# RWKV-7 main loop: the small output products of a group of four chunks behind the products for N, instead of one pair in each state step

## The chip, the cores and the metric

The kernel runs on one core of one Trainium2 chip. The metric is the device time of one execution in microseconds (us), lower is better. Before the change three executions took 1460.63, 1456.24 and 1459.01 us, median 1459.01.

The engines are named as the profile names them: PE is TensorE (matrix products), PEld its weight loads, DVE is VectorE, ACT is ScalarE, POOL is GpSimd, SP issues most of the DMAs. PSUM is the memory into which TensorE writes; here it has eight banks, four of them for large projections (tiles `dp`) and four for everything else (pool `mx`).

## The reference

The program is one layer of a decoder: an input projection, three mixers side by side (HGRN2, a dilated-window attention, RWKV-7), an output projection, a gated MLP and a gated embedding. Only the RWKV-7 mixer matters here. Its recurrence, per head of width 64 over 1024 positions, is

```
def step(state, inp):
    r_t, w_t, k_t, v_t, kk_t, a_t = inp
    sa = jnp.einsum('bhvk,bhk->bhv', state, -kk_t)
    state = (state * w_t[:, :, None, :] + sa[..., None] * (kk_t * a_t)[:, :, None, :]
             + v_t[..., None] * k_t[:, :, None, :])
    return state, jnp.einsum('bhvk,bhk->bhv', state, r_t)
```

with four heads. `y`, the second result, is then normalised, gated and passed on to the output projection.

## The kernel before

The recurrence is computed in chunks of 64 positions, 16 chunks in a row. Two heads make a pair that fills the 128 partitions, so the loop runs twice (p = 0 and p = 1, the first and the second head pair). `rwkv_groups` handles four chunks at a time, groups g = 0 to 3. For a group it computes what does not need the state for all four chunks together, and then walks through four state steps u = 0 to 3, chunk c = 4g + u.

Around the steps these tiles matter:

- `W` holds, per chunk and head, two 128x64 blocks: slot 0 makes the part of the output that comes from inside the chunk, slot 1 the part of the next state that does. `XV` holds the corrected values. Both are complete before the products for N.
- `pn` (L958): eight products `W[.., 1, :]` by `XV`, 64x64 results, two heads by four chunks. VectorE scales them into `N` (L959).
- `GM`: per chunk a 128x256 matrix, of which columns 128 to 255 carry the state on and columns 0 to 127 turn the state into output. VectorE writes it in two halves of two chunks (L949).
- One state step: `pS = GM . S` (L975), then on VectorE `S' = pS * gC + N` (L976). For the output: a pair of products `W[.., 0, :]` by `XV`, one for each head, into `pyo` (L978), and `GM . S` added to it (L980).
- In group 0 step 0 has no state: `S` is a copy of `N` (L971), and there is only the pair. Chunk 15 has no pS.

Between the steps TensorE is given other work by hand: `fill(1)` takes the next three products (128x512) of a projection that belongs to a later stage (L130, L132, L134); `inverse_first` (L872) starts the inverse of the next group, `values_turn` transposes the next group's v (L844). After a group, `place` copies the transposed v into XV on ScalarE (L851), which must wait until all readers of the old XV are through, and `result` copies `pyo` out of its bank (L885). Then come the scores of the next group, `sc` (L903), and `pu` (L914).

The loop stands under `manual_schedule` for TensorE, VectorE, ScalarE and GpSimd, so the order there is the order of the code; pieces of a later projection are put between by a scheduler (the weight splits L106 and L108 and some L130 to L134). The four banks of pool `mx` are handed out as tiles are asked for: which bank a tile gets, and thus whom it waits for, follows from the tiles before it.

Of the kernel before, what the change touches and what calls it, by code (L numbers as in the profile page):

```python
# [10 lines left out]
F32 = mybir.dt.float32  # L11
# [7 lines left out]
P = 128  # L19
# [60 lines left out]
class Trunk:  # L80
# [708 lines left out]
    def rwkv_groups(self, p, rp, d, y3, steps):  # L789

        nc, mxp = self.nc, self.mxp
        ar, v, gC = d["ar"], d["v"], d["gC"]
        msk = self.msk.rearrange("p (m h i) -> p m h i", h=2, i=64)
        Q = slice(0, 64), slice(64, 128)

        def rt(name, shape, bufs=1):
            return rp.tile(shape, F32, tag=name, name=self.nm(name), bufs=bufs)

        def fill(k):
            for _ in range(k):  # L800
                next(steps)
# [13 lines left out]
        def quad(name, g):  # L815
            t[name, g] = w = rt(name, [P, 4, P])
            nc.vector.tensor_tensor(w.rearrange("p u (o i) -> p u o i", i=32),
                                    d[name][:, group(g), :].unsqueeze(2).broadcast_to([P, 4, 4, 32]),
                                    self.qmask.rearrange("p (o i) -> p o i", i=32).unsqueeze(1).broadcast_to([P, 4, 4, 32]),
                                    ALU.mult)  # L820
# [12 lines left out]
        def add_ar(g):  # L833
            nc.gpsimd.tensor_copy(add[:, :, 0, :], ar[:, group(g), 1, :])
# [18 lines left out]
        X, GM = rt("X", [P, 4, P]), rt("GM", [P, 4, 256])  # L853
        GM5 = GM.rearrange("p u (a h i) -> p u a h i", a=2, h=2)
        W, XV = rt("W", [P, 4, 2, 2, 64]), rt("XV", [P, 4, 2, 64])
# [12 lines left out]
        def inverse_first(g):  # L868
            t["Y"] = rt("Y", [P, 4, P])
            py = mxp.tile([P, 4, P], F32, tag="mx", name=self.nm("py"))  # L870
            for u in range(4):
                nc.tensor.matmul(py[:, u, :], t["AB", g][:, u, :], t["T", g][:, u, :], start=True, stop=True)  # L872
            nc.scalar.copy(t["Y"], py)
            if g < 3:
                scores_bd(g + 1)

        def values_turn(g):
            t["pv"] = turn(lambda b: v[:, 256 * g + P * b:256 * g + P * b + P])
# [8 lines left out]
        S, before = None, None  # L887
# [3 lines left out]
        for g in range(4):  # L891
# [55 lines left out]
            def gm(us):  # L947
                for h, q in enumerate(Q):
                    nc.vector.tensor_tensor(GM5[q, us, :, h, :], pg[q, us], add[q, us], ALU.add)  # L949
# [8 lines left out]
                    nc.tensor.matmul(pn[q, u, :], W[:, u, h, 1, :], XV[:, u, h, :], start=True, stop=True)  # L958
            nc.vector.tensor_tensor(N, pn, gC[:, cs].unsqueeze(2).broadcast_to([P, 4, 64]), ALU.mult)  # L959
            gm(slice(2, 4))  # L960
            if not last:
                add_ar(g + 1)
            self.pending("w")
            fill(1)
            py = mxp.tile([P, 4, 64], F32, tag="mx", name=self.nm("pyo"))
            for u in range(4):
                c = 4 * g + u
                Sn = None
                if S is None:
                    Sn = rt("S", [P, 64], bufs=3)  # L970
                    nc.vector.tensor_copy(Sn, N[:, u, :])  # L971
                elif c < 15:
                    Sn = rt("S", [P, 64], bufs=3)
                    pS = mxp.tile([P, 64], F32, tag="mx", name=self.nm("pS"))
                    nc.tensor.matmul(pS, GM[:, u, 128:256], S, start=True, stop=True)  # L975
                    nc.vector.scalar_tensor_tensor(Sn, pS, gC[:, c:c + 1], N[:, u, :], ALU.mult, ALU.add)  # L976
                for h, q in enumerate(Q):
                    nc.tensor.matmul(py[q, u, :], W[:, u, h, 0, :], XV[:, u, h, :], start=True, stop=S is None)  # L978
                if S is not None:
                    nc.tensor.matmul(py[:, u, :], GM[:, u, 0:128], S, start=False, stop=True)  # L980
                S = Sn
                if u == 0:
                    fill(1)
                if u == 1:
                    if last:
                        self.rwkv_norm_in(p, d, 0, (3,))
                        fill(1)
                    else:
                        inverse_first(g + 1)
                        if g == 2:  # L990
                            self.rwkv_norm_in(p, d, 0, (1,))
                        quad("U", g + 1)
                if u == 2 and not last:
                    values_turn(g + 1)
                    fill(1)
# [944 lines left out]
```

## Time and profile before

| | us |
|---|---|
| three executions | 1456.24, 1459.01, 1460.63 |
| profiled execution, its span (its own time is shown by nothing else) | 1457.3 |
| first head pair's loop, groups 0 to 3: first L958 | 158.8, 175.2, 191.8, 209.2 |
| second head pair's loop, groups 0 to 3: first L958 | 346.1, 362.5, 379.1, 396.6 |
| last L980 of the second head pair | 402.4 |

The times in the last three rows are starts, counted from the span's start. The two loops take about 60 us each with all that stands between the steps. In four stretches of the loops the engines were busy as follows (columns: stretch, its length, then busy us and instructions of PE, PEld, DVE, ACT, POOL; then the granted clock of TensorE, the share of the DMA engines, GB/s):

```profile
157.00:167.00 10.00, 10.00 (x87) 8.30 (x86) 4.70 (x11) 4.04 (x12) 5.99 (x6) 1.00 0.13 38
173.00:184.00 11.00, 11.00 (x93) 9.55 (x93) 4.44 (x12) 3.53 (x12) 3.35 (x5) 1.00 0.01 2
...
378.00:389.00 11.00, 10.85 (x94) 9.12 (x93) 9.31 (x19) 7.37 (x20) 6.46 (x6) 1.00 0.28 65
394.00:404.00 10.00, 9.79 (x76) 7.81 (x75) 4.99 (x13) 2.14 (x7) 3.43 (x4) 1.00 0.37 107
```

A product of float32 operands appears in the profile as two passes, each with its own weight load, so `x4` at L978 is one pair. A row of the timeline merges passes of one kind that follow each other: its start is that of the first pass, and its length reaches to the end of the last, which overlaps with the start of what follows. What a group costs TensorE is therefore read from start to start.

### The profile page before, as it was taken

To read this page: it belongs to the slowest core of one execution; us is meant where nothing else is said; L and a number is where in the kernel's file an instruction comes from. 1 tells how busy PE (TensorE), PEld (TensorE's weight loads), DVE (VectorE), ACT (ScalarE), POOL (GpSimd) and SP (SyncE) were. 2 spreads that over 40 slices of the span, in tenths; PEclk is the share of its full clock that TensorE was granted. 3 is DMA by queue.
4 is the path that set the end of the run, shared out by engine and by line. 5 is a ranking of instruction groups with operands and counts; after the bars stand their busy time and mean duration, and the time that the engine had idled before them with its cause. 6 is when DMAs were issued, how large, how long until landed. Compare 5 with 4: busy or idle time off the path is not lost.

```text
span 1457.3 us, 20344 instructions
## 1 busy us (share of the span) xinstructions
PE 1428.6 (98%) x7480; PEld 1176.0 (81%) x7480; DVE 1102.4 (76%) x1672; ACT 634.7 (44%) x1131; POOL 449.2 (31%) x364
## 2 busy tenths in 40 slices
PE   9999999999999999899999999999999999999996
PEld 7888887888877777787888888888888888888885
DVE  6567566684777689637798889888888799777685
ACT  6531343213434565335554434444444444455552
POOL 2332432323421132222145445444454000002342
PEclk9999999999999999999999999999999999999998
DMA  5223021240251220165323332333333883351443
GB/s 214 70 80 116 30 73 58 66 130 30 65 196 52 109 73 28 65 224 205 145 97 114 109 97 99 110 101 108 105 98 122 314 283 96 103 166 58 126 156 116
DMA packets 80019, 167.84 MB, mean 115 GB/s; under 512 B 20080, under 2 KB 22256, under 8 KB 79920
## 3 DMA queue, kind: packets, MB, share of 16 engines
q1 hardware_dynamic: 65568, 145.44, 30.4%
q10 hardware_dynamic: 13408, 17.57, 3.6%
q0 software_dynamic: 944, 3.54, 0.7%
q8 instruction: 59, 0.97, 0.3%
q14 instruction: 40, 0.33, 0.1%
HBM read 120.12 MB, written 46.40 MB: 114 GB/s over the span
## 4 chain that ended last, share of the span: by engine, by line
PE 86%; DVE 6%; issue 3%; ACT 2%; POOL 1%; DMA 1%; SPq 0%; DVEq 0%; ACTq 0%; POOLq 0%
PE bg L1395 16%; PE bv L1395 12%; PE dp L130 8%; PE dp L132 8%; PE dp L134 8%; PE bg L1713 7%; PE bv L1713 7%; PE hsc L1073 1%; PE bv L130 1%; PE bv L134 1%; PE bv L132 1%; PE bg L130 1%; PE bg L134 1%; PE bg L132 1%; PE swq L1230 1%
## 5 line engine op out<-in xcount | busy, mean ns | idle before, releaser
L130 PE MATMUL dp<-xh,whi 128*128 128x512 f32 x544 | 197.7, 408 | 1.6 <-ACT xh L375 1.6
L132 PE MATMUL dp<-xl,whi 128*128 128x512 f32 x544 | 188.5, 392 | 0.3 <-DVE xl L376 0.3
L134 PE MATMUL dp<-xh,wlo 128*128 128x512 f32 x544 | 188.6, 392 | 0.0
L108 POOL TENSOR_TENSOR wlo<-wraw,whi 128x512 fp32r<-128x512 f32 x63 | 90.8, 1445 | 223.7 <-ACT whi L106 205.2
L108 POOL TENSOR_TENSOR wlo<-raw,whi 128x512 fp32r<-128x512 f32 x84 | 135.8, 1635 | 75.5 <-ACT whi L106 75.5
L1395 PE MATMUL bg<-t,whi 128*128 128x512 f32 x352 | 132.5, 389 | 0.6 <-DVE ct L1598 0.6
L106 ACT CAST whi<-wraw 128x512 fp32r<-128x512 f32 x120 | 72.5, 618 | 129.2 <-PE dp L132 86.8
L130 PEld LDWEIGHTS dp<-xh,whi 128*128 128x128 f32 x544 | 101.7, 189 | 24.0 <-issue 3.3
L134 PEld LDWEIGHTS dp<-xh,wlo 128*128 128x128 f32 x544 | 102.3, 188 | 22.4 <-issue 0.5
L132 PEld LDWEIGHTS dp<-xl,whi 128*128 128x128 f32 x544 | 102.5, 189 | 20.3 <-DVE xl L376 0.6
L108 POOL TENSOR_TENSOR wlo<-s,whi 128x512 fp32r<-128x512 f32 x44 | 66.5, 1511 | 161.2 <-ACT whi L106 161.2
L1713 PE MATMUL bg<-t,whi 128*128 128x512 f32 x308 | 94.9, 389 | 0.0
L1713 PE MATMUL bv<-t,whi 128*128 128x512 f32 x308 | 94.8, 389 | 0.0
L106 ACT CAST whi<-raw 128x512 fp32r<-128x512 f32 x88 | 52.7, 619 | 91.4 <-issue 48.5
L106 ACT CAST whi<-s 128x512 fp32r<-128x512 f32 x66 | 39.0, 621 | 122.0 <-PE bg L1395 113.4
L175 POOL TENSOR_TENSOR rst<-rst,mhalf 128x4 f32<-128x4 f32 (+1 forms) x9 | 10.2, 1132 | 223.7 <-DVE rst L173 223.7
L1395 PEld LDWEIGHTS bg<-t,whi 128*128 128x128 f32 x352 | 66.0, 188 | 14.7 <-ACT whi L106 1.0
L108 DVE TENSOR_TENSOR wlo<-wraw,whi 128x512 fp32r<-128x512 f32 x57 | 48.8, 855 | 38.1 <-ACT whi L106 33.7
L1709 ACT CAST t<-t 128x512 fp32r<-128x512 f32 x77 | 47.8, 622 | 47.9 <-PE bv L1713 35.4
L1713 PEld LDWEIGHTS bv<-t,whi 128*128 128x128 f32 x308 | 57.8, 188 | 12.0
L1713 PEld LDWEIGHTS bg<-t,whi 128*128 128x128 f32 x308 | 57.7, 188 | 12.0
L1395 PE MATMUL bg<-t,wlo 128*128 128x512 f32 x176 | 67.2, 389 | 0.0
(426 smaller groups left out, 3613.9 us busy)
## 6 DMA issues: line engine op xcount, KB each, us to landing
raw<-in_ffn_up_dram SPq DMA_DIRECT2D x44, 512.0 KB, 3.7
wraw<-in_w_in_dram SPq DMA_DIRECT2D x29, 512.0 KB, 3.8
z<-zst SPq DMA_DIRECT2D x18, 512.0 KB, 3.0
gb<-ct SPq DMA_DIRECT2D x33, 256.0 KB, 2.3
t<-gb SPq DMA_DIRECT2D x33, 256.0 KB, 2.9
t<-gt SPq DMA_DIRECT2D x33, 256.0 KB, 2.7
zl<-z SPq DMA_DIRECT2D x16, 512.0 KB, 4.5
wraw<-in_ple_gate_dram SPq DMA_DIRECT2D x16, 512.0 KB, 3.6
```

Source lines behind the costliest of these rows:

```text
L106: nc.scalar.copy(hi, src)
L108: eng.tensor_tensor(lo, src, hi.bitcast(F32), ALU.subtract)
L130: nc.tensor.matmul(ps[hf], wh, xh[hf], start=first, stop=False)
L132: nc.tensor.matmul(ps[hf], wh, xl[hf], start=False, stop=False)
L134: nc.tensor.matmul(ps[hf], wl, xh[hf], start=False, stop=last)
L175: nc.gpsimd.tensor_tensor(r2[:, :n], r[:, :n], self.mhalf[:, :n], ALU.pow)
L1073: nc.tensor.matmul(sc[:, c, :], ks[:, c * P:(c + 1) * P], view(qt, c * P, [2 * n, 64 // n], [HT + n, 2], [1, n]), start=True, stop=True)
L1230: nc.tensor.matmul(pq[h][:, b:b + w], d["q"][hs, qb * P:nk], d["k"][hs, b:b + w], start=True, stop=True)
L1395: nc.tensor.matmul(ps, w[part == 2][:, s], X[k][part == 1], start=start and k == part == 0, stop=k == 3 and part == 2, skip_group_check=no ...
L1709: nc.scalar.copy(xh, x)
L1713: nc.tensor.matmul(ps[m], wt[part == 2][:, m * P:(m + 1) * P], (xh, xl)[part == 1], start=k == part == 0, stop=k == NK - 1 and part == 2)
```

## The change

All eight products of L978 are issued for the whole group directly behind the eight of `pn`, before the first fill. `start=True` is given only for the first chunk of each head (u = 0): the bank is opened once, and the later chunks write their own columns of it without opening it again. In the steps only `GM . S` is left to add (now L982; pS is now L979 and the state L980). The tile `pyo` is asked for one fill earlier.

```diff
             nc.vector.tensor_tensor(N, pn, gC[:, cs].unsqueeze(2).broadcast_to([P, 4, 64]), ALU.mult)
             gm(slice(2, 4))
+            py = mxp.tile([P, 4, 64], F32, tag="mx", name=self.nm("pyo"))
+            for u in range(4):
+                for h, q in enumerate(Q):
+                    nc.tensor.matmul(py[q, u, :], W[:, u, h, 0, :], XV[:, u, h, :], start=u == 0, stop=S is None and u == 0,
+                                     skip_group_check=True)
             if not last:
                 add_ar(g + 1)
             self.pending("w")
             fill(1)
-            py = mxp.tile([P, 4, 64], F32, tag="mx", name=self.nm("pyo"))
             for u in range(4):
                 c = 4 * g + u
                 Sn = None
...
                     nc.tensor.matmul(pS, GM[:, u, 128:256], S, start=True, stop=True)
                     nc.vector.scalar_tensor_tensor(Sn, pS, gC[:, c:c + 1], N[:, u, :], ALU.mult, ALU.add)
-                for h, q in enumerate(Q):
-                    nc.tensor.matmul(py[q, u, :], W[:, u, h, 0, :], XV[:, u, h, :], start=True, stop=S is None)
                 if S is not None:
-                    nc.tensor.matmul(py[:, u, :], GM[:, u, 0:128], S, start=False, stop=True)
+                    nc.tensor.matmul(py[:, u, :], GM[:, u, 0:128], S, start=False, stop=True, skip_group_check=True)
                 S = Sn
```

On TensorE, first head pair, group 1, from the products for N to the second step's pS, there stood before (line, operation, output from inputs, size of the output, count):

```order
L958 MATMUL pn_1565<-XV_1261,W_1260 64x64 x8
L130 MATMUL dp_1578<-xh_105,whi_1410 128x512
L132 MATMUL dp_1578<-xl_106,whi_1410 128x512
L134 MATMUL dp_1578<-xh_105,wlo_1412 128x512
L975 MATMUL pS_1586<-S_1460,GM_1259 128x64
L978 MATMUL pyo_1584<-XV_1261,W_1260 64x64 x2
L980 MATMUL pyo_1584<-S_1460,GM_1259 128x64
L130 MATMUL dp_1578<-xh_89,whi_1410 128x512
L132 MATMUL dp_1578<-xl_90,whi_1410 128x512
L134 MATMUL dp_1578<-xh_89,wlo_1412 128x512
L975 MATMUL pS_1596<-S_1585,GM_1259 128x64
```

And at the same place now:

```order
L958 MATMUL pn_1565<-XV_1261,W_1260 64x64 x8
L964 MATMUL pyo_1577<-XV_1261,W_1260 64x64 x8
L130 MATMUL dp_1587<-xh_105,whi_1419 128x512
L132 MATMUL dp_1587<-xl_106,whi_1419 128x512
L134 MATMUL dp_1587<-xh_105,wlo_1421 128x512
L979 MATMUL pS_1594<-S_1462,GM_1259 128x64
L982 MATMUL pyo_1577<-S_1462,GM_1259 128x64
L130 MATMUL dp_1587<-xh_89,whi_1419 128x512
L132 MATMUL dp_1587<-xl_90,whi_1419 128x512
L134 MATMUL dp_1587<-xh_89,wlo_1421 128x512
L979 MATMUL pS_1602<-S_1593,GM_1259 128x64
```

Eight products now stand ahead of the first fill, and pS and the state's part of the output follow each other directly.

On TensorE, at the end of group 0 of the first head pair, the turn to the next group, with the engines whose signals an instruction waits for (- before, + now):

```order
-L975 MATMUL pS_1461<-S_1447,GM_1259 128x64 [waits DVE_49]
-L978 MATMUL pyo_1421<-XV_1261,W_1260 64x64 x2
-L980 MATMUL pyo_1421<-S_1447,GM_1259 128x64
+L979 MATMUL pS_1463<-S_1451,GM_1259 128x64 [waits DVE_49]
+L982 MATMUL pyo_1409<-S_1451,GM_1259 128x64
 L844 MATMUL pt_1472<-cst,ar_483 128x128 [waits Activation_49]
 L844 MATMUL pt_1472<-cst,ar_483 128x128
-L903 MATMUL sc_1483<-ar_483,kbd_1274 128x128 [waits DVE_49]
+L903 MATMUL sc_1483<-ar_483,kbd_1274 128x128 [waits PE_49,Activation_49]
```

The scores `sc` waited for VectorE's last state, whose bank they took. They now get the bank of v's transpose and wait for ScalarE's last copy of it into XV. The same is so at the turn from group 1 to 2 and at both turns of the second head pair; at the turns from group 2 to 3 `sc` waits as before.

On VectorE, first head pair, group 2, the first three states, the masks for the next group (L817) and half of the split of a later projection's weight (L108) stood so before:

```order
L976 SCALAR_TENSOR_TENSOR S_1764<-pS_1765,gC_805,N_1738 128x64
L976 SCALAR_TENSOR_TENSOR S_1774<-pS_1775,gC_805,N_1738 128x64
L817 TENSOR_TENSOR U_1789<-Tc_901,cst 128x512
L108 TENSOR_TENSOR wlo_2050<-wraw_2046,whi_2048 128x512
L976 SCALAR_TENSOR_TENSOR S_1791<-pS_1792,gC_805,N_1738 128x64
```

And now:

```order
L980 SCALAR_TENSOR_TENSOR S_1772<-pS_1773,gC_805,N_1738 128x64
L108 TENSOR_TENSOR wlo_2050<-wraw_2046,whi_2048 128x512
L980 SCALAR_TENSOR_TENSOR S_1780<-pS_1781,gC_805,N_1738 128x64
L817 TENSOR_TENSOR U_1793<-Tc_901,cst 128x512
L980 SCALAR_TENSOR_TENSOR S_1795<-pS_1796,gC_805,N_1738 128x64
```

The split moved ahead of the second state. In the second head pair it stays where it was. The rows of ScalarE, GpSimd and SP stand in the same order as before, and so does TensorE behind the two loops.

## The prediction

> **What bounds the kernel now.** I read the page first (span, busy shares, chain), then the tiles of the state step, then the timeline of TensorE, VectorE and ScalarE through four of the eight groups, and last the waits of TensorE over the whole run.
>
> ```profile
> span 1457.3 us, 20344 instructions
> PE 1428.6 (98%) x7480; PEld 1176.0 (81%) x7480; DVE 1102.4 (76%) x1672; ACT 634.7 (44%) x1131; POOL 449.2 (31%) x364
> PE 86%; DVE 6%; issue 3%; ACT 2%; POOL 1%; DMA 1%; SPq 0%; DVEq 0%; ACTq 0%; POOLq 0%
> ...
> PE hsc L1073 <- DVE qt L1078: 4.6, 4, 2.1
> ```
>
> TensorE is busy 98% of the span and carries 86% of the chain that ended last. The last row is the largest group of its waits in the whole run: 4.6 us in 4 waits. So TensorE's own time is nearly the kernel's time, and what is taken out of its stream comes off the end, unless a new wait takes its place.
>
> The products that the change moves are the pairs of L978. They are counted by tile:
>
> ```profile
> L978 PE MATMUL pyo<-XV,W x128: 222/246/271, 160.3 to 402.1; 128*64 128x64 f32 x128
> L975 PE MATMUL pS<-S,GM x56: 217/274/294, 161.5 to 401.1; 128*128 128x64 f32 x56
> L958 PE MATMUL pn<-XV,W x128: 222/222/271, 158.8 to 397.0; 128*64 128x64 f32 x128
>   PE pS L975: 16.4, 20
> ```
>
> Each product appears as two passes, so 128 rows are 64 products or 32 pairs: 2 head pairs, 4 groups, 4 steps. The fourth row is from the tile S: VectorE, which makes the next state, sat idle 16.4 us in 20 of its 28 steps until pS was there. Mostly VectorE waits for TensorE in this loop. Group 1 of the first head pair shows how TensorE passes through it:
>
> ```profile
> 175.19 0.69 PE L958 MATMUL pn<-XV,W 128*64 128x64 f32 x16
> 175.81 0.50 PE L130 MATMUL dp<-xh,whi 128*128 128x512 f32 x1
> ...
> 176.61 0.33 PE L975 MATMUL pS<-S,GM 128*128 128x64 f32 x2
> 176.87 0.34 PE L978 MATMUL pyo<-XV,W 128*64 128x64 f32 x4
> 177.13 0.43 PE L980 MATMUL pyo<-S,GM 128*128 128x64 f32 x2
> 177.37 0.48 PE L130 MATMUL dp<-xh,whi 128*128 128x512 f32 x1
> ...
> 178.15 0.33 PE L975 MATMUL pS<-S,GM 128*128 128x64 f32 x2
> ...
> 178.95 1.11 PE L872 MATMUL py<-T,ABt 128*128 128x128 f32 x8
> 179.90 0.33 PE L975 MATMUL pS<-S,GM 128*128 128x64 f32 x2
> ...
> 180.69 0.39 PE L844 MATMUL pt<-cst,v 128*128 128x128 f32 x2
> ...
> 181.62 0.33 PE L975 MATMUL pS<-S,GM 128*128 128x64 f32 x2
> ...
> 182.42 0.39 PE L844 MATMUL pt<-cst,ar 128*128 128x128 f32 x2
> 182.81 0.89 PE sc L903 x8
> ```
>
> The columns are start, length, engine, line. Nothing is idle here. From pS to whatever follows L980 the four steps take 0.76, 0.80, 0.79 and 0.80 us (177.37 less 176.61, and so on), mean 0.79. The last row is from the chain: 8 wide passes in a row take 0.89, or 0.111 each. A pair alone takes 0.26 (176.87 to 177.13) for passes that in pn follow each other at (0.69 - 0.222) / 15 = 0.031. The difference is what a change between narrow and wide products costs here, and each step pays it twice.
>
> **The change, part by part.**
>
> *Added.* Eight products, 16 narrow passes, behind the 16 of pn in each of 8 groups. The change of kind is already paid by pn, so I take 16 x 0.031 = 0.50 us a group, 4.0 in all. The bounds are 0.50 and the whole of pn with its end, 175.19 to 175.81, 0.62 (5.0 in all); I take the lower because the runs adjoin. That a bank is opened once and the later pairs add into it is a flag on the same instructions; I cost it at nothing, and the first rival says what it costs if that is wrong.
>
> *Removed from 28 full steps.* Without the pair, pS and L980 are four wide passes in a row, 4 x 0.111 = 0.445. A step saves 0.79 - 0.445 = 0.34; 28 save 9.6. The lower bound is the pair's own 0.26, 7.3.
>
> *Removed from the two first steps* (group 0, no state yet), where the pair stands between two wide products of a projection:
>
> ```profile
> 160.01 0.40 PE L134 MATMUL dp<-xh,wlo 128*128 128x512 f32 x1
> 160.34 0.34 PE L978 MATMUL pyo<-XV,W 128*64 128x64 f32 x4
> 160.61 0.50 PE L130 MATMUL dp<-xh,whi 128*128 128x512 f32 x1
> 160.94 0.39 PE L132 MATMUL dp<-xl,whi 128*128 128x512 f32 x1
> ...
> 156.63 0.23 PE dp L130
> ```
>
> 160.01 to 160.94 is 0.93 for two wide products and the pair; undisturbed such products follow at 0.23 (the last row, from the chain), so 0.47 goes in each, 0.9 in both.
>
> *Removed from the two last steps* (chunk 15 has no pS), here of the second head pair:
>
> ```profile
> 401.46 0.28 DVE L976 SCALAR_TENSOR_TENSOR S<-pS,gC,N 128x64 f32<-128x64 f32 x1 [0.67 <-PE pS L975]
> 401.61 0.43 PE L980 MATMUL pyo<-S,GM 128*128 128x64 f32 x2
> 401.98 0.34 PE L978 MATMUL pyo<-XV,W 128*64 128x64 f32 x4
> 402.24 0.30 PEld L980 LDWEIGHTS pyo<-S,GM 128*128 128x128 f32 x2
> 402.49 0.48 PE L130 MATMUL dp<-xh,whi 128*128 128x512 f32 x1
> ```
>
> L980, pair, L980 take 401.61 to 402.49, 0.88. With the pair gone the second L980 waits for the state: VectorE ends at 401.74, TensorE sees it 0.14 later (a row of group 2, below, has that length), and two passes of 0.111 end at 402.10. That saves 0.39, 0.8 for both, and this product is then late by the state instead of the pair.
>
> Removed together: 9.6 + 0.9 + 0.8 = 11.3. Less the 4.0 added: 7.3.
>
> *New waits.* First, the scores of the next group (L903) now take the bank in which v's transpose lay, so they wait until ScalarE has copied it into XV. This is so at four turns, groups 0 to 1 and 1 to 2 of both head pairs; at the other two it is pu, later, that waits.
>
> ```profile
> 181.17 0.26 ACT L851 COPY XV<-pt 64x128 f32<-64x128 f32 x1 [0.44 <-PE pt L844]
> 182.30 0.83 ACT L851 COPY XV<-pt 64x128 f32<-64x128 f32 x3 [0.87 <-PE pyo L978]
> ...
> 182.65 1.06 PE L903 MATMUL sc<-ar,kbd 128*128 128x128 f32 x8
> ```
>
> Before, three of the four copies waited for the last pair, which read the old XV; that wait goes. The copies then run from 181.17 without a gap, 0.26 + 0.83 and a little between, to 182.28, and with 0.14 for the signal the bank is free at 182.42. TensorE, its last step shorter by 0.34, is at L903 at 182.31. I take 0.1 a turn, 0.4 in all; the bounds are 0 and 0.34, the step's whole gain, 1.4 in all. Behind L903 stand a projection's products and pu, and VectorE's masks wait for it, so what is lost here is lost.
>
> Second, group 2, where VectorE also splits a weight (shown for the second head pair):
>
> ```profile
> 382.49 0.28 DVE L976 SCALAR_TENSOR_TENSOR S<-pS,gC,N 128x64 f32<-128x64 f32 x1 [0.60 <-PE pS L975]
> 382.69 1.19 DVE L817 TENSOR_TENSOR U<-Tc,cst 128x512 f32<-128x512 f32 x1
> 383.81 1.76 DVE L108 TENSOR_TENSOR wlo<-wraw,whi 128x512 fp32r<-128x512 f32 x1
> 385.49 0.27 DVE L976 SCALAR_TENSOR_TENSOR S<-pS,gC,N 128x64 f32<-128x64 f32 x1
> 385.90 0.41 PE L975 MATMUL pS<-S,GM 128*128 128x64 f32 x2
> ```
>
> Queued behind the 1.76 us split is the state of step 2, and pS of step 3 waits for it (385.76 to 385.90 is the signal). VectorE's row of work hangs on pS of step 1, which comes 0.50 - 0.34 = 0.16 later than now. So pS of step 3 comes at 386.06 instead of 0.52 earlier (three steps of 0.34 less 0.50): 0.7 of the gain is lost. In the first head pair the order puts the split ahead of step 1's state. There VectorE has 0.60 idle to give (the first row), so of 1.76 that state comes 1.16 late; pS of step 2 asks for it 1.1 after it was ready (group 1: a state made from 178.52 in 0.28, asked for at 179.90). I take 0.1 for this group, 0.8 for both; the bounds are 0 and 1.4.
>
> Third, six products now wait for two signals instead of one, with an instruction of TensorE's queue for the second, some 0.05 each: 0.3. The other queues keep their order; no DMA is moved on any of them. ScalarE's copies of XV, xr and y only come earlier.
>
> Sum: 11.3 - 4.0 - 0.4 - 0.8 - 0.3 = 5.8 us. Against the profiled execution, span 1457.3, that makes 1451.5. No time around that span is shown; it lies 1.7 under the median 1459.0 and inside the runs, 1456.2 to 1460.6. From the median: **1453.2**.
>
> **The rivals.**
>
> *The moved run does not pack.* From its second pair on it adds into an open bank, which no narrow row before does in a row. If each pair kept its 0.26, a group would pay 1.04, all groups 8.3, and 11.3 - 8.3 - 1.5 leaves 1.5: 1457.5. Against it speaks pn, the same shapes and the same tile XV, at 0.031 a pass. The Trainium skill, page "TensorE: Matmul & The Clock Gate", section "LDWEIGHTS (loading the stationary operand)", has a rule that speaks for a milder form: a weight load takes its columns divided by 1.2 in ns, so 64 columns would need 53 ns each, an estimate from that page. By that rule 16 passes would cost 0.85 a group, 6.8 in all, and the time would be 1456.0; the trace disagrees, as pn's 16 passes at 0.031 each show.
>
> *The state sets the pace in half of the steps.* If VectorE were late in 14 steps as it is in group 2, their 0.34 would turn into waits: 5.8 - 4.8 leaves 1.0, 1458.0. For it: only 20 of 28 steps had VectorE idle. Against it: in group 1 the state of step 1 is ready at 178.80 (the row below), and TensorE asks for it at 179.90.
>
> ```profile
> 178.52 0.28 DVE L976 SCALAR_TENSOR_TENSOR S<-pS,gC,N 128x64 f32<-128x64 f32 x1 [0.76 <-PE pS L975]
> ```
>
> *The time is taken up later.* Some stage after 402 us may wait for something other than TensorE, and the gain ends there: 1459. The waits of 4.6 us and less speak against it, and so does the equal order behind the loop.
>
> *Slower.* The state sets the pace in every step: the pairs only filled time in which TensorE had to wait for S, and the 0.50 ahead of the first step delays the whole chain. Then nothing is won, and 4.0 + 1.5 is added: 1464.5. It decides from the point where S is ready less than 0.34 ahead of its pS; that margin is 1.1 by the row above, and only in group 2 is it gone.
>
> **How the numbers follow.** Forecast, 1453.2: 0.62. The run does not pack: 0.10. State in part of the steps: 0.15. Taken up later: 0.08. Slower: 0.05. About 0.3%, or 4.4 us, is what a measurement of this kernel tells from no change. The forecast alone is beyond it: faster 0.62; the next three are within: 0.33; slower 0.05. The range starts at the best sum, no new wait, 7.3: 1451.7. The other end takes the dearer bounds: 7.3 + 0.9 + 0.8 removed, 5.0 added and 1.4 + 1.4 + 0.3 of waits leave 0.9, 1458.1, and the rivals at 1457.5 and 1458.0 lie inside. The runs shown lie 1.6 above and 2.8 below their median; with 1.7 of that below and 0.4 above I give 1450.0 to 1458.5.
>
> **What would show it.** Right: L964 with 16 passes directly behind pn, from the first L964 to the wide product behind it about 0.6; pS to the product behind L982 near 0.45 in groups 0, 1 and 3; the XV copies four in a row, without the wait for pyo; in group 2 pS of step 3 still behind VectorE. Wrong: a run of L964 near 1 us or longer; pS waiting for S in groups 0, 1 or 3; L903 idle by more than 0.3; or these all as said and a later wait of TensorE longer by the same amount.

## The result, and the profile after

Four executions of the changed kernel took 1449.28 to 1453.59 us, median 1451.59; four of the kernel before beside them 1456.24 to 1461.25, median 1459.82. The ratio is 0.9947, 95% interval 0.9929 to 0.9965: 8.2 us between the medians. Two later sets with the same kernel gave 0.9955 (0.9942 to 0.9969) and 0.9944 (0.9932 to 0.9956). The forecast was 1453.2, a gain of 5.8, and the range 1450.0 to 1458.5.

From the page of the changed kernel, span and busy shares:

```profile
span 1447.5 us, 20343 instructions
PE 1418.8 (98%) x7480; PEld 1171.2 (81%) x7480; DVE 1101.9 (76%) x1672; ACT 634.7 (44%) x1131; POOL 448.5 (31%) x364
```

The count of passes is the same, 7480, but TensorE is busy 9.8 us less. TensorE still bounds the kernel.

Next the tiles: the moved products, and what the tile S says of VectorE's waiting (us, times).

```profile
L964 PE MATMUL pyo<-XV,W x128: 222/222/222, 160.0 to 391.5; 128*64 128x64 f32 x128
...
  PE pS L979: 11.7, 17
```

All 128 passes of the pairs are now L964. VectorE waited for pS 16.4 us before and 11.7 now: its room has shrunk, but most states still wait for TensorE.

TensorE's timeline of group 1 of the first head pair (start, length, engine, line; a bracket has the idle time before the row and what ended it), and one row of group 2 of the second:

```profile
174.74 0.69 PE L958 MATMUL pn<-XV,W 128*64 128x64 f32 x16
175.25 0.64 PE L964 MATMUL pyo<-XV,W 128*64 128x64 f32 x16
175.82 0.50 PE L130 MATMUL dp<-xh,whi 128*128 128x512 f32 x1
...
176.63 0.33 PE L979 MATMUL pS<-S,GM 128*128 128x64 f32 x2
176.79 0.39 PE L982 MATMUL pyo<-S,GM 128*128 128x64 f32 x2
176.99 0.47 PE L130 MATMUL dp<-xh,whi 128*128 128x512 f32 x1
...
180.43 0.33 PE L979 MATMUL pS<-S,GM 128*128 128x64 f32 x2
...
180.81 0.39 PE L844 MATMUL pt<-cst,ar 128*128 128x128 f32 x2
181.14 1.16 PE L903 MATMUL sc<-ar,kbd 128*128 128x128 f32 x8
...
380.50 0.41 PE L979 MATMUL pS<-S,GM 128*128 128x64 f32 x2 [0.98 <-DVE S L980]
```

The run stands behind pn, and from its start to the wide product it takes 0.57. From pS to what follows L982 is 0.36 and 0.38 in the two steps shown (176.99 less 176.63, 180.81 less 180.43), and 0.38 in the mean of the four, where it was 0.79 before. From the last transpose to `sc` is 0.33 (180.81 to 181.14); before it was 0.23 (182.42 to 182.65). The last row is the wait that the prediction had put into group 2 of the second head pair.

ScalarE's copies of v's transpose at that turn:

```profile
179.98 1.11 ACT L851 COPY XV<-pt 64x128 f32<-64x128 f32 x4
```

Four copies in a row, without the wait for pyo. TensorE's waits over the whole run (us in total, times, longest):

```profile
PE pgm L945 <- DVE X L936: 1.0, 1, 1.0
PE pS L979 <- DVE S L980: 1.0, 1, 1.0
```

These two stand in the loops; before, the one at pgm was 0.2. The largest of the run, 4.6 at `hsc`, is as before.

Now the loops piece by piece. "Steps" runs from the first pass of pn to the first of the next `sc` (in group 3 to the first transpose of the result, `yt`), "head" from `sc` to pn; all are differences of starts on TensorE, worked out from its timeline (us).

| | g0 | g1 | g2 | g3 | sum |
|---|---|---|---|---|---|
| steps before, pair 1 / pair 2 | 7.19 / 7.19 | 7.45 / 7.46 | 7.91 / 7.91 | 8.51 / 7.38 | 61.0 |
| steps after | 6.08 / 6.08 | 6.40 / 6.40 | 6.38 / 7.60 | 7.13 / 6.59 | 52.7 |
| heads before | 9.97 / 9.09 | 9.17 / 9.17 | 9.17 / 9.16 | 9.51 / 9.57 | 74.8 |
| heads after | 9.97 / 9.08 | 9.17 / 9.18 | 9.16 / 9.17 | 10.44 / 9.28 | 75.5 |

The two loops took 68.88 + 66.94 = 135.8 before and 64.74 + 63.37 = 128.1 now: 7.7 less. One product of a projection (0.23) moved from group 3 of the first head pair to behind the loop, so with the same work it is 7.5. In three further profiled executions of this order (the kernel again twice, and `open_each` below) they took 128.0 to 128.3. The spans differ by 9.8; the other 2.1 lie outside the loops: up to the first `sc` and between the loops it is 0.9 longer now, behind them 3.0 shorter (last section).

### The profile page after: what moved, and what is told of

The parts are those of the page before. It is cut to its first block, busy times and chain, and to the rows that moved or that the text cites. A ratio compares the mean times of both kernels' runs of the same rounds, so it can differ in the third digit from the quotient of the medians.

```text
span 1447.5 us, 20343 instructions
## 1 busy us (share of the span) xinstructions
PE 1418.8 (98%) x7480; PEld 1171.2 (81%) x7480; DVE 1101.9 (76%) x1672; ACT 634.7 (44%) x1131; POOL 448.5 (31%) x364
## 4 chain that ended last, share of the span: by engine, by line
PE 87%; DVE 5%; issue 3%; ACT 2%; POOL 2%; DMA 1%; SPq 0%; DVEq 0%; ACTq 0%; POOLq 0%
PE bg L1397 16%; PE bv L1397 12%; PE dp L130 8%; PE dp L132 8%; PE dp L134 8%; PE bg L1715 7%; PE bv L1715 7%; PE hsc L1075 2%; PE bv L130 1%; PE bv L134 1%; PE bv L132 1%; PE bg L130 1%; PE bg L134 1%; PE bg L132 1%; PE swq L1232 1%
## 5 line engine op out<-in xcount | busy, mean ns | idle before, releaser
L134 PE MATMUL dp<-xh,wlo 128*128 128x512 f32 x544 | 188.6, 392 | 0.0
L108 POOL TENSOR_TENSOR wlo<-wraw,whi 128x512 fp32r<-128x512 f32 x63 | 90.8, 1444 | 224.1 <-ACT whi L106 193.2
L108 POOL TENSOR_TENSOR wlo<-raw,whi 128x512 fp32r<-128x512 f32 x84 | 135.7, 1634 | 75.6 <-ACT whi L106 75.6
L134 PEld LDWEIGHTS dp<-xh,wlo 128*128 128x128 f32 x544 | 102.5, 189 | 21.9 <-issue 0.2
L108 POOL TENSOR_TENSOR wlo<-s,whi 128x512 fp32r<-128x512 f32 x44 | 66.1, 1503 | 161.3 <-ACT whi L106 161.3
L106 ACT CAST whi<-raw 128x512 fp32r<-128x512 f32 x88 | 52.7, 619 | 91.1 <-issue 48.2
L108 DVE TENSOR_TENSOR wlo<-wraw,whi 128x512 fp32r<-128x512 f32 x57 | 47.9, 840 | 38.8 <-ACT whi L106 34.4
```

The costliest lines, as they stand in the source:

```text
L106: nc.scalar.copy(hi, src)
L108: eng.tensor_tensor(lo, src, hi.bitcast(F32), ALU.subtract)
L134: nc.tensor.matmul(ps[hf], wl, xh[hf], start=False, stop=last)
```

## The experiments

Theory: a step pays for a visit of TensorE from wide to narrow products and back, and the change drops 32 such visits for 8 runs that join one which is there already. Rivals: only the place between pS and the state's part of the output (L980) counts; XV and the banks coming free early is what gains; opening the bank once is what makes the run cheap; a pair costs the same wherever it stands.

Three sets, each on one chip with its own executions of the kernel before (medians 1456.84, 1457.47 and 1457.82): the first four rows, the next four and the last three. "Loops" is the sum of both loops in the profiled execution, with as many projection products in it as the changed kernel has (group 3 of the first head pair holds one to three more or less in some orders, 0.23 us each); by this count the kernel before has 135.6.

| kernel | median us | ratio to before, 95% | loops us |
|---|---|---|---|
| after_again | 1450.51 | 0.9955 (0.9942 to 0.9969) | 128.3 |
| no_pairs | 1448.88 | 0.9944 (0.9931 to 0.9956) | 126.8 |
| pair_first | 1457.93 | 1.0007 (0.9998 to 1.0016) | 136.0 |
| run_apart | 1452.04 | 0.9964 (0.9951 to 0.9976) | 129.9 |
| open_each | 1450.49 | 0.9955 (0.9942 to 0.9967) | 128.2 |
| run_twice | 1453.05 | 0.9969 (0.9957 to 0.9980) | 130.5 |
| masks_late | 1449.44 | 0.9942 (0.9930 to 0.9955) | 127.4 |
| masks_late_x | 1449.64 | 0.9947 (0.9934 to 0.9961) | 127.3 |
| pair_twice | 1459.90 | 1.0015 (1.0006 to 1.0024) | 138.3 |
| after_b | 1449.55 | 0.9944 (0.9932 to 0.9956) | 128.0 |
| masks_late_b | 1448.39 | 0.9936 (0.9922 to 0.9949) | 127.4 |

Within a set, the interval of every edit of the changed kernel overlaps that of the changed kernel's order itself (`after_again`, `open_each`, `after_b`), so the times alone do not set them apart. What follows is read from the steps in the traces, which in the changed kernel agree from one execution to the next to 0.02 us.

**The changed kernel again**, unedited, in the first and the third set:

> The changed kernel once more, on the same chip as the three below. Theory A (every visit to narrow products between wide ones costs a change of kind on TensorE, and 32 such visits were taken away): 7 to 8 us less than before, ratio about 0.995, with the two loops shorter by 7.5 us in the trace and the rest of the 9.8 us between the two profiled executions gone, since there one had a stretch of half clock near 490 us that the other did not have. Rival (a third of the gain stands behind the loops and is real): the stages behind 402 us again 3 us shorter than before.

> The changed kernel itself, beside the kernel with the late masks on one chip. 0.9955 of before, as in the first set (0.9942 to 0.9969).

Both came out as the first result did.

**The pair ahead of pS**: the kernel before, each pair moved out from between pS and the state.

```diff
@@ kernel before
                 c = 4 * g + u
                 Sn = None
+                for h, q in enumerate(Q):
+                    nc.tensor.matmul(py[q, u, :], W[:, u, h, 0, :], XV[:, u, h, :], start=True, stop=S is None)
...
-                for h, q in enumerate(Q):
-                    nc.tensor.matmul(py[q, u, :], W[:, u, h, 0, :], XV[:, u, h, :], start=True, stop=S is None)
```

> The kernel before with each step's pair ahead of pS instead of between pS and the state's part: as many visits to narrow products as before (32), but none between pS and its partner. Theory A: within 1 us of before, ratio 1.000. Rival B (the cost lies in standing between pS and the state's part of the output, which then follow each other directly): most of the gain, ratio 0.995 to 0.996. Rival C (the gain comes from XV and the banks coming free early): 1.000, as XV is still read in every step.

Nothing was gained, 1.0007. Its TensorE timeline, group 1, one step:

```profile
176.35 0.40 PE L134 MATMUL dp<-xh,wlo 128*128 128x512 f32 x1
176.67 0.34 PE L970 MATMUL pyo<-XV,W 128*64 128x64 f32 x4
176.94 0.43 PE L977 MATMUL pS<-S,GM 128*128 128x64 f32 x2
177.21 0.39 PE L980 MATMUL pyo<-S,GM 128*128 128x64 f32 x2
```

The price is paid in gaps: 0.32 from the wide product to the pair where wide ones follow at 0.23, 0.27 for the pair, and 0.27 from pS to L980 where the changed kernel has 0.16. That is 0.47 for the visit, no less than on the other side of pS (0.41), so the place between pS and L980 was not what counted. Nor is it any change of product: where the wide passes of L872 follow wide ones and pS follows them (178.95 to 179.90 in the prediction's rows), eight take 0.95, with no such gap.

**The pair twice**: the kernel before with each pair issued twice in its step.

```diff
@@ kernel before
-                for h, q in enumerate(Q):
-                    nc.tensor.matmul(py[q, u, :], W[:, u, h, 0, :], XV[:, u, h, :], start=True, stop=S is None)
+                for h, q in (*enumerate(Q), *enumerate(Q)):
+                    nc.tensor.matmul(py[q, u, :], W[:, u, h, 0, :], XV[:, u, h, :], start=True, stop=True)
```

> The kernel before, with each pair of small products issued twice in its state step (the second time it writes the same values into a bank opened anew, so the output is the same); nothing else is moved. It tells apart what a visit of TensorE to narrow products costs from what their passes cost. Theory A (a visit costs about 0.27 us beyond its passes, and a further pass in the same visit 0.031): the pair of L978, now 8 passes, adds 4 x 0.031 = 0.12 a step, 3.5 to 4.0 us in 32 steps: ratio to before 1.0026, and from pS to what follows L980 0.90 to 0.93 instead of 0.79. Rival B (a pair costs its 0.26 wherever it stands; the changed kernel gains from something else): 0.26 a step, 8.3 us, ratio 1.0057, and 1.05 from pS to what follows L980.

Its TensorE timeline, same step:

```profile
176.51 0.33 PE L975 MATMUL pS<-S,GM 128*128 128x64 f32 x2
176.77 0.45 PE L978 MATMUL pyo<-XV,W 128*64 128x64 f32 x8
...
177.40 0.48 PE L130 MATMUL dp<-xh,whi 128*128 128x512 f32 x1
```

From pS to what follows L980 is 0.89 instead of 0.76 in this step: four more passes cost 0.13, 0.03 each, as in theory A. The pair's 0.26 would give 1.02. In all it cost 2.1 us and not 3.5 to 4, though the loops grew by 2.7: the steps of groups 0, 1 and 3 are 0.35 to 0.47 longer for the same work, but those of both groups 2 only 0.07 and 0.08, since TensorE waits for VectorE's split there in any case.

**The run apart**: the changed kernel with the run behind the first fill, so that it stands between wide products.

```diff
@@ changed kernel
-            for u in range(4):
-                for h, q in enumerate(Q):
-                    nc.tensor.matmul(py[q, u, :], W[:, u, h, 0, :], XV[:, u, h, :], start=u == 0, stop=S is None and u == 0,
-                                     skip_group_check=True)
             if not last:
                 add_ar(g + 1)
             self.pending("w")
             fill(1)
+            for u in range(4):
+                for h, q in enumerate(Q):
+                    nc.tensor.matmul(py[q, u, :], W[:, u, h, 0, :], XV[:, u, h, :], start=u == 0, stop=S is None and u == 0,
+                                     skip_group_check=True)
```

> The changed kernel with the run of eight products behind the first fill instead of directly behind pn: one visit of its own per group, nothing else moved on any engine. Theory A: 8 visits, each 0.25 to 0.35 us beyond its passes, 2.0 to 2.8 us slower than the changed kernel, ratio 0.9965. Rivals B and C (not the visits, but what the pairs stood between or kept occupied): as the changed kernel, 0.9947.

Its TensorE timeline, group 1:

```profile
175.63 0.69 PE L968 MATMUL pyo<-XV,W 128*64 128x64 f32 x16
...
176.51 0.39 PE L982 MATMUL pyo<-S,GM 128*128 128x64 f32 x2
```

From the first L958 (174.12) to L982 is 2.39 here and 2.05 in the changed kernel (174.74 to 176.79): 0.34 for one more visit, with the same products. XV is read for the last time before the first step here too, so its coming free early is not what gains. The whole came out below the 2.0 to 2.8 that were expected: the medians differ by 1.5, the loops by 1.7. The steps grew by 0.34 or 0.35 in five of the eight groups and by 0.22 or 0.23 in groups 0, but not in group 2 of the second head pair, where TensorE waits for VectorE in any case, and the wait at pgm in group 3 of the first became 0.5 shorter. The visit is shown as a price of its own, some 0.3.

**Each pair opens the bank**: the flag alone. Chunks 0 to 2 of each group are expected to lose their within-chunk part; the output is not the reference's.

```diff
@@ changed kernel
-                    nc.tensor.matmul(py[q, u, :], W[:, u, h, 0, :], XV[:, u, h, :], start=u == 0, stop=S is None and u == 0,
+                    nc.tensor.matmul(py[q, u, :], W[:, u, h, 0, :], XV[:, u, h, :], start=True, stop=S is None and u == 0,
```

> The changed kernel, but each of the four pairs of the run opens the bank again, instead of the first alone; the order of every engine is the same. Chunks 0 to 2 of each group lose their within-chunk part in the output. Theory A (opening is a flag and costs nothing): the run of 16 passes at L964 takes 0.64 to 0.69 us as in the changed kernel, each group's steps 6.1 to 6.4, and the time is that of the changed kernel within 0.9 us, ratio to before 0.9955. Rival B (what makes the run cheap is that later pairs add into an open bank; each opening costs a visit of its own): a pair alone took 0.26 in the kernel before and takes 0.12 in the run, so 4 x 0.14 = 0.5 more in each group, 4 us in all: ratio 0.998.

0.9955, and the steps are those of the changed kernel to 0.02 us. Opening the bank once or four times makes no difference to the time; it only makes the order possible.

**No pairs**: the changed kernel without the run, but for the pair of the first chunk in each head pair. So 60 of the 64 products are left out, not 62 as the expectation says.

```diff
@@ changed kernel
-            for u in range(4):
+            if S is None:
                 for h, q in enumerate(Q):
-                    nc.tensor.matmul(py[q, u, :], W[:, u, h, 0, :], XV[:, u, h, :], start=u == 0, stop=S is None and u == 0,
-                                     skip_group_check=True)
+                    nc.tensor.matmul(py[q, 0, :], W[:, 0, h, 0, :], XV[:, 0, h, :], start=True, stop=True, skip_group_check=True)
...
-                    nc.tensor.matmul(py[:, u, :], GM[:, u, 0:128], S, start=False, stop=True, skip_group_check=True)
+                    nc.tensor.matmul(py[:, u, :], GM[:, u, 0:128], S, start=g > 0 and u == 0, stop=True, skip_group_check=True)
```

> Leaves out the part of the output that comes from inside the chunk, for all chunks but the first: 62 of 64 small products are not issued at all. Theory A, with the run behind pn at 0.031 us a pass: 8 x 0.50 = 4.0 us less than the changed kernel, so 11.5 less than before, ratio 0.992. Rival (the run behind pn costs as much as visits of its own, 4 x 0.26 a group): 8 us less than the changed kernel, ratio 0.989.

A miss: only 1.6 us were saved. TensorE in group 1:

```profile
173.57 0.69 PE L958 MATMUL pn<-XV,W 128*64 128x64 f32 x16
174.18 0.50 PE L130 MATMUL dp<-xh,whi 128*128 128x512 f32 x1
...
175.89 0.40 PE L134 MATMUL dp<-xh,wlo 128*128 128x512 f32 x1
176.19 0.43 PE L978 MATMUL pS<-S,GM 128*128 128x64 f32 x2
176.47 0.39 PE L981 MATMUL pyo<-S,GM 128*128 128x64 f32 x2
```

From pn to the wide product is 0.61, and 1.08 with the run (174.74 to 175.82): at its place the run costs 0.47. But pS of the second step then comes 0.30 behind L134 instead of 0.24, and L981 0.28 behind pS instead of 0.16. The steps are 0.29 shorter (6.11), and 0.18 has become waiting, for a first state that stands behind GM on VectorE. In groups 0, which keep one pair, the steps are as long as with the run (6.08). In group 2 of the first head pair VectorE's order went back to that of before, and the steps took 7.60 instead of 6.38. The time of this kernel therefore doesn't measure the run.

**The run twice**: the price from the other side. The output has the within-chunk part twice.

```diff
@@ changed kernel
+            for u in range(4):
+                for h, q in enumerate(Q):
+                    nc.tensor.matmul(py[q, u, :], W[:, u, h, 0, :], XV[:, u, h, :], start=False, stop=S is None and u == 0,
+                                     skip_group_check=True)
             if not last:
                 add_ar(g + 1)
```

> The changed kernel with the run of the eight small products issued a second time behind the first, so the output has the within-chunk part twice. It measures the price of the run by adding it. Theory A (16 passes of 0.031 us with nothing that hides them; the first run showed 0.47 at its place): 8 x 0.47 = 3.8 us over the changed kernel, ratio to before 0.998, steps of groups 0, 1 and 3 longer by 0.45 to 0.50 each. Rival B (the run lies partly beside other work, as the kernel without the pairs seemed to say, which was only 1.6 us under the changed one): 1 to 2 us over, ratio 0.9965, steps longer by 0.1 to 0.3.

TensorE in group 1:

```profile
174.50 0.64 PE L964 MATMUL pyo<-XV,W 128*64 128x64 f32 x16
174.97 0.64 PE L968 MATMUL pyo<-XV,W 128*64 128x64 f32 x16
175.54 0.50 PE L130 MATMUL dp<-xh,whi 128*128 128x512 f32 x1
```

0.47 for the second run, and the steps of groups 1 are 0.47 longer, as theory A has it (0.33 in groups 0). The total is 2.6 above `open_each` and the loops are 2.3 above it, between the two expectations. VectorE's order moved too: the steps of the seven other groups grew by 3.0 in all, those of group 2 of the second head pair became 0.75 shorter, and the head of group 3 behind them 0.75 longer (a wait at pgm). What is missing from 3.0 is the head of group 3 of the first head pair, 0.73 shorter: there TensorE comes later and waits less at pgm.

**The masks late**: the changed kernel, VectorE's masks (L817) behind the third state instead of the second.

```diff
@@ changed kernel
                         if g == 2:
                             self.rwkv_norm_in(p, d, 0, (1,))
-                        quad("U", g + 1)
                 if u == 2 and not last:
+                    quad("U", g + 1)
                     values_turn(g + 1)
```

> The changed kernel with the four-part masks of the next group (VectorE, L817) made after the third state step instead of the second, so that in group 2 the state is not queued behind both the masks and the split of a weight. Theory A (the one wait of TensorE for the state that is left in the loop, 0.98 us in group 2 of the second head pair, is VectorE's queue): that wait goes, these steps take 6.5 to 6.7 instead of 7.6, and the time is 0.9 to 1.1 under the changed kernel, ratio to before 0.9948. Rival B (VectorE has no room anywhere: the masks then stand in front of something else): the wait returns at pu of the next group, which needs the masks, and the time is within 0.4 of the changed kernel.

> The kernel with the late masks again, beside the changed kernel. If the 0.7 to 0.9 us by which its two loops were shorter are there in every execution, it stands 0.5 to 1.3 us under the changed kernel; if they come from one profiled execution, within 0.4.

The 0.98 us wait is gone, and the steps there take 6.73 instead of 7.60. In the first head pair, where there was no such wait, the steps of group 2 take 6.72 instead of 6.38. TensorE's waits in this kernel:

```profile
PE pgm L945 <- DVE X L936: 0.7, 2, 0.4
...
PE sc L903 <- DVE S L980: 0.5, 2, 0.3
```

Two new small waits for VectorE, at `sc` at the turn from group 2 to 3 of both head pairs, and a second one at pgm, in the second head pair, take part of it back. Of the loops 0.6 to 0.8 us are left, in both profiled executions, and the medians stand 1.1 and 1.2 under those of the changed order in the same sets. It is faster than the kernel before by 8.0 and 9.4 us; its lead over the changed kernel lies inside the intervals.

**X by ScalarE too**: as above, and in group 3 of the first head pair, where TensorE waits at pgm, ScalarE makes VectorE's half of X.

```diff
@@ masks_late
-            for q, copy in zip(Q, (nc.scalar.copy, nc.vector.tensor_copy)):
+            for q, copy in zip(Q, (nc.scalar.copy, nc.scalar.copy if g == 3 and p == 0 else nc.vector.tensor_copy)):
```

> The kernel with the late masks, and in group 3 of the first head pair the second half of the copy of px into X is made by ScalarE instead of VectorE. In the changed kernel TensorE waits 0.99 us there at pgm for VectorE, whose queue is held by a split that waits for a weight. Theory A (part of the gain of group 2 is given back at this one wait): pgm starts about 0.9 earlier, the stretch from sc to pn of this group falls from 10.4 to about 9.5, and the time is 1.8 to 2.1 under the changed kernel, ratio to before 0.994. Rival B (the whole neighbourhood runs at the pace of the weight's transfer, so the next wait takes it): the stretch is shorter, the steps behind it longer, and the time is that of the kernel with the late masks alone.

The head fell from 9.77 to 9.17, but the steps behind it grew from 7.12 to 8.21: 0.69 of this is three projection products that moved there, 0.40 is waiting. VectorE there:

```profile
205.66 1.22 DVE L476 TENSOR_TENSOR zst<-zst,dp 128x1024 f32<-128x1024 f32 x1 [1.57 <-ACT zst L471]
206.79 0.85 DVE L949 TENSOR_TENSOR GM<-pgm,addend 64x256 f32<-64x256 f32 x2
```

pgm started at 204.17, but GM now stands behind a piece of the normalisation that waits for ScalarE, and TensorE waits for GM. The loops are 0.1 shorter for the same work, and the median is that of the late masks: rival B, most of the wait moves on.

## Why the prediction was right, point by point

**What bounds.** Right: TensorE's own time went, and the time followed it. The rivals in which the state sets the pace, in half of the steps or in all, fell: pS waits for the state once, 0.98 us. So did the one in which the time is taken up later: behind the loops nothing became longer.

**The number.** Predicted were 5.8 us; measured are 7.5 in the loops for the same work, and 8.2 between the medians (6.3 and 8.3 in the two later sets with the changed kernel unedited). The prediction's best sum, no new wait, was 7.3 and 1451.7. The median 1451.59 lies just beyond it, and inside the range because of the 1.7 that was put on for scatter, not because the sum reached it.

**The added run.** Predicted 0.50 a group, measured 0.47 at its place (`no_pairs` and `run_twice`). It joined the visit of pn. The rival that it does not pack fell. The 0.031 a pass is a mean: the passes start two at a time, and the twos stand 0.06 apart (174.85, 174.91, 174.96 in pn of the changed kernel). So the trace speaks against adding up all loads one behind the other, not against the 53 ns for one load that the prediction sets beside it.

**The 28 full steps.** The mechanism was right, the term 28 x 0.34 = 9.6 was too small. It put the four wide passes that stay at 4 x 0.111, the pace of the passes of `sc`. L982 keeps that pace: its row is 0.39 long for passes of 0.275, so its two stand 0.11 apart. But the two passes of pS take 0.16 (176.63 to 176.79), the first of them only 0.06, as its row is 0.33 long for passes of 0.274; and a projection's product follows 0.09 behind the last pass. The short first pass was there before the change, in the 0.33 of pS in the prediction's rows. It is not the number of columns: pS and L982 both have 64. Why the first pass is cheaper was not tried. A step keeps 0.38 and not 0.445, and saves 0.41: 11.5 us. Taken apart by `pair_twice`, 0.12 of the 0.41 are the passes and some 0.29 the change of kind, there and back. The Trainium skill, page "TensorEngine Tiling (Array Packing)", section "Key Properties", says that changing the tiling mode drains TensorE. The gaps around the pairs agree with it; the page gives no price, and here it is about 0.3 us a visit.

**The turn to the next group.** Right: 0.10 at `sc`, predicted 0.1. Group 1 closes on it: 4 x 0.41 less 0.47 less 0.10 is 1.07, measured 1.05. So the second signals, 0.3 in all in the prediction, were not seen here beside the 0.10; the groups 0 and group 3 of the first head pair close to 0.02 without them as well.

**The two last steps.** For the third and the last step together the prediction has 0.34 + 0.39 = 0.73. In the first head pair they save 0.80, a projection's products counted out. In the second they save 0.45, from the third pS to the wide product behind the last L982 (1.40 before, 401.09 to 402.49, and 0.95 now). Here the step failed. TensorE in the second head pair, group 3:

```profile
394.73 0.33 PE L979 MATMUL pS<-S,GM 128*128 128x64 f32 x2
394.90 0.39 PE L982 MATMUL pyo<-S,GM 128*128 128x64 f32 x2
395.44 0.43 PE L982 MATMUL pyo<-S,GM 128*128 128x64 f32 x2 [0.15 <-DVE S L980]
395.68 0.48 PE L130 MATMUL dp<-xh,whi 128*128 128x512 f32 x1
```

The prediction took L980 and the state from their places before, 401.61 and 401.74. But the third step's pair goes as well, so L982 now stands 0.17 behind pS where L980 stood 0.52, while VectorE starts the state 0.37 behind pS in both kernels. The 0.35 that the third step gains is waited for again at the last L982, which has nothing in front of it. In the first head pair two products of a projection stand there.

**Group 2, second head pair.** Right, on VectorE as predicted:

```profile
378.39 1.77 DVE L108 TENSOR_TENSOR wlo<-wraw,whi 128x512 fp32r<-128x512 f32 x1
380.09 0.27 DVE L980 SCALAR_TENSOR_TENSOR S<-pS,gC,N 128x64 f32<-128x64 f32 x1
```

The steps gained 0.31 of the 1.17 that the new sizes give (4 x 0.41 less 0.47), so 0.86 was lost to the wait; predicted 0.7.

**Group 2, first head pair.** Here the step failed: 0.1 was to be lost, and the steps gained 1.53, 0.36 more than the 1.17. The prediction let the split take its 1.76 ahead of the second state. VectorE after (and one row from a time when GpSimd is idle), then before; GpSimd after, then before:

```profile
193.02 0.84 DVE L108 TENSOR_TENSOR wlo<-wraw,whi 128x512 fp32r<-128x512 f32 x1
...
200.92 0.69 DVE L108 TENSOR_TENSOR wlo<-wraw,whi 128x512 fp32r<-128x512 f32 x1 [1.74 <-ACT whi L106]
```

```profile
196.52 1.76 DVE L108 TENSOR_TENSOR wlo<-wraw,whi 128x512 fp32r<-128x512 f32 x1
```

```profile
193.28 4.63 POOL L108 TENSOR_TENSOR wlo<-wraw,whi 128x512 fp32r<-128x512 f32 x3
```

```profile
194.78 4.62 POOL L108 TENSOR_TENSOR wlo<-wraw,whi 128x512 fp32r<-128x512 f32 x3
```

Moved forward, the split begins before GpSimd's three splits and takes 0.84; before, it lay wholly beside them and took 1.76. So the wait that the kernel before had in this group (its steps were 0.45 longer than those of group 1) went as well. The duration of a VectorE row was taken along to a place where GpSimd was not yet busy. The Trainium skill, page "SBUF — State Buffer", section "SBUF: two separate sides", says that VectorE with two inputs in SBUF and a GpSimd operation that reads SBUF exclude each other for a whole instruction; these rows agree, 0.69 alone and 1.76 beside GpSimd. Other runs bear it out: in `no_pairs` the split of this group fell back in among GpSimd's (193.56), took 1.77, and the steps were 7.6; in `run_twice` it began ahead of them in both head pairs and took 0.68. That this is the cause was read from such rows, not tested alone.

**Given back later.** The prediction had no term for it. Group 3's head in the first head pair grew by 0.9, at pgm. ScalarE, in the changed kernel:

```profile
200.27 0.62 ACT L106 CAST whi<-wraw 128x512 fp32r<-128x512 f32 x1 [0.94 <-DMA wraw<-in_w_in_dram]
```

At this `sc` TensorE stands 3.0 us earlier than before (199.72 before, 196.69 now), but the cast of the weight starts only 2.1 earlier (202.36 before, 200.27 now): it waits for the transfer, VectorE's split (the row at 200.92 above) for the cast, and the copy of X (205.56) stands behind 4 us of other work that VectorE does after the split without a gap. `masks_late_x` shows that this neighbourhood doesn't give the time back when one copy is taken away.

**The sum.** Steps by the new sizes: 11.5 + 0.9 + 0.8 removed, 8 x 0.47 = 3.8 added, 0.4 at `sc`, which leaves 9.0. Group 2 takes 0.86 and gives 0.36; one projection product moved from the steps of group 3 behind the loop, 0.23; the last state of the second head pair takes 0.35. That is 8.4; measured were 61.0 less 52.7, or 8.3. The heads took 0.6 back, which leaves 7.7, or 7.5 for the same work, where 5.8 was predicted. The difference has the size of the one term that was too small, 11.5 instead of 9.6. That the smaller ones cancel is luck: for the prediction's sum 0.2 at the run, 0.3 in group 2 and 0.3 of second signals, against it 0.35 at the last state and 0.6 at the heads.

## What to carry to other kernels

Count the visits of TensorE to a kind of product, not only its passes: a pair of narrow products between wide ones cost 0.40 us, of which 0.12 were passes, and moved into a run of its own kind it cost 0.12. Price the passes that stay where they stand: the first and the last of a short row cost less than the mean pass of a long one. When gains are added up step by step, place each step where the gains ahead of it have put it, and ask then whether what it waits for has come. Where one engine gets ahead by some us, look for the next transfer that doesn't move with it, and price the duration of a VectorE instruction together with what GpSimd does at that time.

## What the runs showed of the hardware

TensorE's clock falls to half in some executions of one and the same kernel and not in others, at a place where it had stood idle twice just before, 0.69 and 1.09 us. Windows of 4 us behind the loops: stretch, length, busy us of PE, PEld, DVE, ACT and POOL, then the granted clock, share of the DMA engines, GB/s. First the kernel before, then the changed kernel as profiled with the result, then the same kernel again:

```profile
488.00:492.00 4.00, 3.31 (x39) 2.68 (x38) 3.44 (x6) 3.96 (x6) 1.50 (x2) 1.00 0.44 141
492.00:496.00 4.00, 2.91 (x15) 2.67 (x14) 0.63 (x2) 2.33 (x6) 0.00 (x0) 0.69 1.02 407
496.00:500.00 4.00, 4.00 (x38) 3.88 (x38) 1.27 (x3) 2.50 (x5) 0.60 (x1) 0.88 0.25 69
```

```profile
484.00:488.00 4.00, 2.49 (x20) 2.20 (x21) 1.46 (x4) 3.45 (x7) 0.00 (x0) 1.00 0.99 384
```

```profile
484.00:488.00 4.00, 2.91 (x16) 2.62 (x15) 0.70 (x3) 2.69 (x7) 0.00 (x0) 0.73 1.01 390
488.00:492.00 4.00, 4.00 (x33) 3.88 (x33) 0.92 (x3) 2.14 (x4) 0.25 (x1) 0.85 0.29 97
```

A clock of 0.69 and 0.88 over 4 us each is 1.7 us of full speed lost, and 0.73 and 0.85 is as much; from 493.6 to 496.9 the granted clock of the kernel before is 0.50, and 1.00 on both sides. This is more than half of the 3.0 us that the first two profiles differ by behind the loops (another 1.3 is one wait of TensorE, for VectorE's `acc`, that only the first has), and it is not the change: with the slower clock in the changed kernel's second execution its span was 1449.1, not 1447.5. The Trainium skill, page "TensorE: Matmul & The Clock Gate", section "What's actually happening", describes free-running windows of about 3.4 us after which an idle TensorE is slowed to half; a stretch of 3.4 us at half the clock would cost that 1.7, an estimate from that page. The length agrees: the clock records of the traces give 3.41 us for each such stretch. But no single idle stretch was that long here. In the clock records the changes lie on a grid of 3.41 us that starts elsewhere in each execution (of the kernel before, the starts of half clock at 8.84 and 493.53 are 142 pieces apart). In the four of the thirteen profiled executions in which the clock fell at this place, both idle stretches lie in one piece of the grid, 1.78 us together; in the other nine the grid parts them, and no piece there holds more than 1.32. That fits a place in the grid as the cause here, which no run tested; at two other places of the program (near 583 and 658 us) the idle time of a piece does not tell, as 1.82 went without a fall and 0.92 with one.

Behind the loops the thirteen executions took 1050.3 to 1051.5 us without such a stretch (six), 1052.2 to 1053.3 with one (six) and 1054.8 with two (`no_pairs`).
